# Forgetting attention's last output weights split ahead of its additions, norm factors spread by one operation and one float32 product, key rotation issued later

## The chip, the cores and the metric

One NeuronCore of a Trainium2 chip runs the whole network in one launch. The metric is the device time of the launch in microseconds; the median of several executions counts. TensorE (PE) multiplies, VectorE (DVE), ScalarE (ACT) and GpSimd (POOL) do the elementwise work, SyncE (SP) issues most transfers.

## The reference

Two layers over 512 tokens of width 1024, float32. Layer 0 is "Forgetting attention" (16 heads of 64, with a decay added to the scores), layer 1 latent attention (16 heads; queries from a latent of 768, keys and values from one of 256, and one rotated key of 64 shared by all heads). A feed-forward block with a convolution over time follows each. Every block begins with an RMS norm.

```python
def rmsnorm(x, g):
    xf = x.astype(jnp.float32)
    y = xf * lax.rsqrt(jnp.mean(xf * xf, axis=-1, keepdims=True) + EPS)
    return (y * g.astype(jnp.float32)).astype(x.dtype)
...
    for layer in range(DEPTH):
        if layer < N_A:
            x = x + fox_mixer(rmsnorm(x, fox_norm[layer]), ...)
        else:
            if layer == N_A:
                k_nope, k_rope, v = mla_shared_kv(x, kv_in_norm, w_dkv, kv_norm, w_uk, w_uv, cos, sin)
            x = x + mla_mixer(rmsnorm(x, mla_norm[j]), w_dq[j], q_norm[j], w_uq[j], ...)
        x = x + conv_ffn(rmsnorm(x, ffn_norm[layer]), ...)
    return rmsnorm(x, final_norm)
```

## The kernel before

Activations lie transposed, features on the 128 partitions and the 512 tokens along the free side, in 8 slabs of 128 features (`xT`). Every float32 operand of a large product is split into a high half (fp32r) and a low half, the rest; `mm3` (lines 83 to 85) makes one product of three: high by high, high by low, low by high. A tile of 128 output features over 1024 inputs is 8 steps of `mm3`, 24 products of 128x128 by 128x512.

Weights come through `load_w`: SP issues the transfer into `raw` (3 buffers), ACT casts the high half into `whi` (L104), DVE, or POOL with `eng=g`, subtracts for the low half `wlo` (L105). `whi` and `wlo` have 2 buffers each, so a tile's weights can be split only when the products of the tile two before are through. With a gain, POOL multiplies the raw weights first (L99).

A scheduler orders each engine's instructions from the program; every engine then runs its list strictly in order, and semaphores make it wait.

**Norms.** `Squares` adds up the squares of the slabs (L139 on ACT or L141 elsewhere, then L145). `rstd_of` sums over features with float32 products against two columns of ones (L153), scales (DVE, L156) and raises to -0.5 (POOL, L158). `bcast` spreads the 512 factors over all partitions: `bcast_ps` splits the factors in two halves (L165, L166), DVE multiplies the identity by each of the four columns of each half (L171, eight operations), and PE multiplies both by ones (L172). ACT copies the result (L179). The norm factor is applied to the result of a tile, not ahead of it (`Rstd.after`): the first tile's end issues the sum, the second's the spread, and tiles that wait for it stand in PSUM (`acc`, 3 buffers).

**Forgetting attention's output projection** is 8 tiles, `wo_tile(d)`. Seven steps of tiles 0 to 4 are done ahead, between the last heads, with weights in spare buffers. `out_proj` (L256) then ends each tile, adds it to `xT` (L264), splits the sum for the feed-forward block (`split_x`: ACT L188, DVE L189) and squares it on POOL, the last on ACT. Tiles 5, 6 and 7 load their weights there, through `whi` and `wlo`.

**Latent attention's entry** (from L633): six query-latent tiles with `down`, then the rotated key's (`wdkv_d[KL]`, called KL below), then two key-value latents. Between them stand the query norm's sum and spread, the latents' scaling and splitting (`latents`, L643, L188, L189), and the key's rotation: `swapped` (ACT, L650), three POOL operations (L751 to L753), a cast (ACT) and a subtraction (POOL). Then come the rotated query part of two heads (`mm_rope`, `turn`), the query tiles `proj_q`, the key tiles `proj_k`, and the first scores (L203).

## Time and profile before

| | us |
|---|---|
| median of 3 runs | 1399.91 (1399.19 to 1400.15) |
| profiled execution, its own time | 1404.06 |
| profiled execution, span of its instructions | 1401.7 |
| PE busy, products | 1371.8 |
| DVE busy | 879.4 |
| ACT busy | 646.4 |
| POOL busy | 281.4 |

The span runs from the first to the last instruction; the execution's own time has what lies around it too. Times of the trace are counted from the span's start. An engine is busy while an instruction of it runs; products are pipelined, so the starts of two products are closer together than one lasts. Line numbers are those of the printed kernel.

### The profile page before, as it was taken

How to read it: one execution, taken by the hardware profiler on the slowest of the kernel's cores; microseconds unless marked ns; L12 is line 12 of the kernel's file. 1: busy time of each engine (PE TensorE's matmuls, PEld its weight loads, DVE VectorE, ACT ScalarE, POOL GpSimd, SP SyncE). 2: the span in 40 equal slices, each digit the busy share in tenths (PEclk: the TensorE clock that was granted, in tenths of full speed). 3: DMA queues.
4: the chain of work that ended last, by engine and by line, in shares of the span. 5: the costliest groups of instructions: out<-in, count | busy, mean ns of one | idle time of the engine just before them, and what ended most of it. 6: DMA issues, size and time to landing. Idle time of an engine off the chain costs nothing.

```text
span 1401.7 us, 17314 instructions
## 1 busy us (share of the span) xinstructions
PE 1371.8 (98%) x6594; PEld 1150.3 (82%) x6594; DVE 879.4 (63%) x1466; ACT 646.4 (46%) x1115; POOL 281.4 (20%) x214
## 2 busy tenths in 40 slices
PE   8999999999999999999899999999999999999997
PEld 7988887788888888887688888888888888888886
DVE  6667786677777654534766565675467777774333
ACT  5588884344444432223456555653244444442111
POOL 4333323300000001244423222212210000000212
PEclk9999999999999999999899999999999999999998
DMA  5321121232232333332121111212322323232331
GB/s 181 104 77 63 57 68 48 90 103 92 96 100 92 104 93 86 100 115 80 42 68 50 62 56 49 76 56 90 105 90 92 104 90 105 91 101 85 98 102 68
DMA packets 41250, 120.21 MB, mean 86 GB/s; under 512 B 5552, under 2 KB 9952, under 8 KB 41168
## 3 DMA queue, kind: packets, MB, share of 16 engines
q1 hardware_dynamic: 39184, 117.00, 26.3%
q0 software_dynamic: 1840, 2.09, 0.6%
q8 instruction: 51, 0.84, 0.2%
q14 instruction: 31, 0.25, 0.1%
q10 hardware_dynamic: 144, 0.03, 0.0%
HBM read 116.74 MB, written 2.36 MB: 85 GB/s over the span
## 4 chain that ended last, share of the span: by engine, by line
PE 44%; DVE 3%; ACT 3%; issue 1%; POOL 0%; DVEq 0%; ACTq 0%
PE acc L84 13%; PE acc L83 13%; PE acc L85 13%; PE att L203 2%; PE acc L730 2%; ACT r L650 1%; ACT e L214 1%; PE att L237 1%; DVE Vp L712 1%; DVE ptl L241 0%; DVE tr L686 0%; DVE r L676 0%; ACT pth L240 0%; DVE r L672 0%; PE att L83 0%
## 5 line engine op out<-in xcount | busy, mean ns | idle before, releaser
L83 PE MATMUL acc<-big,whi 128*128 128x512 f32 (+1 forms) x1504 | 587.6, 391 | 2.7 <-ACT big L188 1.6
L85 PE MATMUL acc<-big,wlo 128*128 128x512 f32 (+1 forms) x1504 | 585.3, 389 | 3.5 <-DVE wlo L105 3.5
L84 PE MATMUL acc<-big,whi 128*128 128x512 f32 (+1 forms) x1504 | 585.5, 389 | 1.2 <-DVE big L189 1.2
L104 ACT CAST whi<-raw 128x1024 fp32r<-128x1024 f32 (+5 forms) x243 | 228.8, 945 | 413.8 <-PE acc L84 289.8
L85 PEld LDWEIGHTS acc<-big,wlo 128*128 128x128 f32 x1504 | 284.2, 189 | 63.0 <-DVE wlo L105 4.1
L83 PEld LDWEIGHTS acc<-big,whi 128*128 128x128 f32 x1504 | 284.0, 189 | 61.2 <-ACT big L188 3.0
L84 PEld LDWEIGHTS acc<-big,whi 128*128 128x128 f32 x1504 | 284.4, 189 | 59.7 <-DVE big L189 1.8
L105 DVE TENSOR_TENSOR wlo<-raw,whi 128x1024 fp32r<-128x1024 f32 (+3 forms) x179 | 232.6, 1299 | 138.6 <-ACT whi L104 136.0
L141 POOL TENSOR_TENSOR r<-xT 128x512 f32<-128x512 f32 x28 | 31.3, 1122 | 724.4 <-DVE xT L264 403.0
L105 POOL TENSOR_TENSOR wlo<-raw,whi 128x768 fp32r<-128x768 f32 (+3 forms) x64 | 107.1, 1677 | 248.3 <-ACT whi L104 135.8
L304 DVE SCALAR_TENSOR_TENSOR c<-u,conv,c 128x510 f32<-128x510 f32 (+1 forms) x176 | 131.1, 748 | 3.5 <-ACT c L302 0.6
L299 DVE TENSOR_TENSOR u<-acc,R 128x512 f32<-128x512 f32 x88 | 60.3, 687 | 76.3 <-PE acc L85 76.3
L214 ACT ACTIVATE e<-e,nm 128x128 f32<-128x128 f32 (+3 forms) x128 | 71.2, 557 | 42.8 <-DVE nm L208 42.8
L145 POOL TENSOR_TENSOR r<-r,r 128x512 f32<-128x512 f32 x38 | 72.5, 1908 | 28.9 <-ACT r L139 22.1
L302 ACT ACTIVATE c<-u,conv 128x512 f32<-128x512 f32 x88 | 71.4, 813 | 3.1 <-DVE u L299 2.7
L308 ACT ACTIVATE sg<-c 128x512 f32<-128x512 f32 x44 | 27.8, 632 | 78.8 <-DVE c L304 78.8
L185 ACT CAST big<-sg 128x512 fp32r<-128x512 f32 x32 | 19.9, 621 | 81.7 <-DVE sg L309 81.6
L217 DVE TENSOR_SCALAR e<-e,rl 128x128 f32<-128x128 f32 (+3 forms) x128 | 56.6, 506 | 1.1
L241 DVE TENSOR_TENSOR ptl<-att,pth 128x512 fp32r<-128x512 f32 (+3 forms) x128 | 53.7, 484 | 5.1 <-ACT pth L240 5.1
L240 ACT CAST pth<-att 128x512 fp32r<-128x512 f32 (+3 forms) x128 | 45.2, 441 | 6.6 <-PE att L237 5.7
L237 PE MATMUL att<-idf,e 128*128 128x128 f32 x320 | 43.4, 275 | 0.5
L237 PEld LDWEIGHTS att<-idf,e 128*128 128x128 f32 x320 | 36.8, 140 | 8.5 <-DVE nm L208 3.8
(183 smaller groups left out, 1460.2 us busy)
## 6 DMA issues: line engine op xcount, KB each, us to landing
raw<-in_wfi SPq DMA_DIRECT2D x88, 512.0 KB, 3.4
raw<-in_wfu SPq DMA_DIRECT2D x32, 512.0 KB, 3.5
raw<-in_wmo SPq DMA_DIRECT2D x16, 512.0 KB, 3.4
raw<-in_wfu SPq DMA_DIRECT2D x16, 384.0 KB, 3.1
raw<-in_wuqn SPq DMA_DIRECT2D x16, 384.0 KB, 3.0
raw<-in_wq SPq DMA_DIRECT2D x8, 512.0 KB, 3.4
raw<-in_wk SPq DMA_DIRECT2D x8, 512.0 KB, 3.4
raw<-in_wv SPq DMA_DIRECT2D x8, 384.0 KB, 3.1
```

Of the source, the lines that this page charges most:

```text
L83: pe.matmul(out, wh, xh, start=start, stop=False)
L84: pe.matmul(out, wh, xl, start=False, stop=False)
L85: pe.matmul(out, wl, xh, start=False, stop=stop)
L104: a.copy(hi[:, c], raw[:, c])
L105: (eng or v).tensor_tensor(out=lo[:, c], in0=raw[:, c], in1=f(hi[:, c]), op=ALU.subtract)
L145: (adder or g).tensor_tensor(out=self.sum, in0=self.sum, in1=sq, op=ALU.add)
L214: a.activation(es[i], es[i], AF.Exp, scale=-1.0, bias=nm[:, i:i + 1], accum_out=l[:, i:i + 1])
L217: v.tensor_scalar(out=es[i], in0=es[i], scalar1=rl[:, i:i + 1], scalar2=None, op0=ALU.mult)
L237: pe.transpose(out=pt[:, (i - j) * P:(i - j + 1) * P], in_=es[i][:, j * P:(j + 1) * P], identity=idf)
L299: v.tensor_tensor(out=u, in0=pt, in1=R, op=ALU.mult)
L302: a.activation(c, u, AF.Identity, scale=cw[:, 2:3], bias=cw[:, 3:4])
L304: v.scalar_tensor_tensor(out=c[:, s:], in0=u[:, :S - s], scalar=cw[:, 2 - s:3 - s], in1=c[:, s:], op0=ALU.mult, op1=ALU.add)
```

## The change

The output projection of the Forgetting attention ends tiles 0 and 1 first, then loads the weights of tiles 5 and 6 (`begun`; tile 5's low half on POOL), then goes on with tiles 2 to 4; its squares are all taken on ACT. A norm's factors are spread by one DVE operation, which multiplies the identity and the factors with broadcast views, and one float32 product against float32 ones. The sum and the spread of an entry norm are issued after 11 and 18 steps of `mm3`, in place of 8 and 16. In the latent attention the query norm's sum and spread are issued inside the key's tile and the first key-value tile, the latents come ahead of the key's rotation, the two key-value squares are summed by PE without an addition, and `turn` issues its DVE operation ahead of the ACT ones.

```diff
@@ -121,8 +121,8 @@
     v.memset(ones, 1.0)
-    ones_r = cp.tile([P, P], F32R, name="ones_r")
+    onesP = cp.tile([P, P], F32, name="onesP")
...
@@ -160,16 +160,10 @@
-        two = T(sp, [P, 2, NT], F32R, "two", 2)
-        rh, rl = two[:, 0, :m], f(two[:, 1, :m])
-        v.tensor_copy(rh, r)
-        v.tensor_tensor(out=rl, in0=r, in1=f(rh), op=ALU.subtract)
-        pt = att()[:, :m * P]
-        for j, part in enumerate((f(rh), rl)):
-            d = T(cp, [P, 512], F32R, "r2", R2)[:, :m * P]
-            for i in range(m):
-                v.tensor_scalar(out=d[:, i * P:(i + 1) * P], in0=idf, scalar1=part[:, i:i + 1], scalar2=None, op0=ALU.mult)
-            pe.matmul(pt, ones_r, d, start=(j == 0), stop=(j == 1))
+        d, pt = r2()[:, :m * P], att()[:, :m * P]
+        v.tensor_tensor(out=d.rearrange("p (i t) -> p i t", i=m), in0=idf.unsqueeze(1).to_broadcast([P, m, P]),
+                        in1=r.unsqueeze(2).to_broadcast([P, m, P]), op=ALU.mult)
+        pe.matmul(pt, onesP, d, start=True, stop=True)
         return pt
...
@@ -253,7 +247,7 @@
-    def out_proj(tile_of, gbase):
+    def out_proj(tile_of, gbase, eng=None):
...
@@ -263,25 +257,27 @@
             split_x(xs, d, xT[:, d, :], None if gbase is None else gain(gbase, d))
-            squares.add(xT[:, d, :], a if d == KD - 1 else g)
+            squares.add(xT[:, d, :], a if d == KD - 1 else (eng or g))
         return xs, squares
...
         def __init__(self, squares):
-            self.squares, self.step, self.R, self.todo = squares, 0, None, []
+            self.squares, self.steps, self.R, self.todo = squares, 0, None, []
+
+        def step(self):
+            self.steps += 1
+            if self.steps == KD + 3:
+                self.r = rstd_of([self.squares.sum], D)
+            if self.steps == 2 * KD + 2:
+                self.R = bcast(self.r)
+                for e in self.todo:
+                    e(self.R)
...
                 self.todo.append(evacuate)
-                if self.step == 0:
-                    self.r = rstd_of([self.squares.sum], D)
-                else:
-                    self.R = bcast(self.r)
-                    for e in self.todo:
-                        e(self.R)
-                self.step += 1
             else:
...
@@ -315,6 +311,7 @@
                         mm3(pt, (wh[:, k, :], wl[:, k, :]), parts(xs, k), k == 0, k == KD - 1)
+                        rstd.step()
                     rstd.after(lambda R, j=j, b=b, pt=pt: evacuate(j, b, pt, R))
...
@@ -576,7 +573,10 @@
-            loads = [(lambda c=c: load(c), KD // 2) for c in (0, 1)] if early else [(lambda: load_w(wfo_d[d], [P, KD, P]), KD)]
+            def whole():
+                return begun.pop(d) if d in begun else load_w(wfo_d[d], [P, KD, P])
+
+            loads = [(lambda c=c: load(c), KD // 2) for c in (0, 1)] if early else [(whole, KD)]
             return pt, out_tile(pt, loads, KD, lambda k: parts(oT, k))
...
@@ -588,7 +588,7 @@
         es = {0: scores(0)}
-        stream, ahead = fillers(), {}
+        stream, ahead, begun = fillers(), {}, {}
...
@@ -615,9 +615,12 @@
                 split_x(oT, h // 2, op_t, None)
-        fill((4,) * 7)
-
-        xs, squares = out_proj(lambda d: ahead[d] if d in ahead else wo_tile(d, acc(), False), G_FFN)
+        fill((4,) * 7 + (0, 1))
+        begun[5] = load_w(wfo_d[5], [P, KD, P], eng=g)
+        begun[6] = load_w(wfo_d[6], [P, KD, P])
+        fill((2, 3, 4))
+
+        xs, squares = out_proj(lambda d: ahead[d] if d in ahead else wo_tile(d, acc(), False), G_FFN, a)
...
@@ -630,11 +633,15 @@
-        def down(w_d, gbase, dst):
+        def down(w_d, gbase, dst, between=()):
             wh, wl = load_w(w_d, [P, KD, P], gain=(KD, gains[:, gbase:gbase + KD]))
             pt = acc()
+            between = dict(between)
             for k in range(KD):
                 mm3(pt, (wh[:, k, :], wl[:, k, :]), parts(xs, k), k == 0, k == KD - 1)
+                rstd.step()
+                if k in between:
+                    between[k]()
             rstd.after(lambda R: v.tensor_tensor(out=dst, in0=pt, in1=R, op=ALU.mult))
...
@@ -668,8 +675,8 @@
             c, t_ = r2(), r2()
+            v.scalar_tensor_tensor(out=c, in0=pt, scalar=MSCALE, in1=cosT, op0=ALU.mult, op1=ALU.mult)
             swapped(t_, pt, MSCALE)
-            v.scalar_tensor_tensor(out=c, in0=pt, scalar=MSCALE, in1=cosT, op0=ALU.mult, op1=ALU.mult)
...
@@ -736,33 +743,41 @@
             down(wdq_d[j], G_MLA, qc[:, j, :])
-            if j:
-                for i in ((0, 1) if j == 1 else (j,)):
+            if j > 1:
+                for i in ((0, 1, 2) if j == 2 else (j,)):
                     squares.add(qc[:, i, :], a, v if j == KQ - 1 else g)
...
         krt, krs = kr[:, 0, :], kr[:, 1, :]
-        down(wdkv_d[KL], G_KVIN, krt)
-        r = rstd_of([squares.sum], QL)
-        down(wdkv_d[0], G_KVIN, qc[:, KQ, :])
-        Rq = bcast(r, T(mp, [P, S], F32, "e3", 2))
+        norm = {}
+
+        def q_sums():
+            norm["q"] = rstd_of([squares.sum], QL)
+
+        def q_factors():
+            norm["R"] = bcast(norm["q"], T(mp, [P, S], F32, "e3", 2))
+
+        down(wdkv_d[KL], G_KVIN, krt, {2: q_sums})
+        down(wdkv_d[0], G_KVIN, qc[:, KQ, :], {0: q_factors})
+        Rq = norm["R"]
         latents(0, KQ - 2, Rq, G_Q)
+        down(wdkv_d[1], G_KVIN, qc[:, KQ + 1, :])
+        mask = T(cp, [P, S], F32, "R", 1)
+        nc.gpsimd.dma_start(mask, const_d[:, C_MM:C_MM + S])
+        kv_sq = []
+        for k in range(KL):
+            kv_sq.append(r2())
+            a.activation(kv_sq[k], qc[:, KQ + k, :], AF.Square)
+        latents(KQ - 2, 2, Rq, G_Q + KQ - 2)
+        end = turn(mm_rope(0))
+        r = rstd_of(kv_sq, KVL)
+        proj_q(0)
         swapped(krs, krt, 1.0)
...
         g.tensor_tensor(out=krt, in0=krt, in1=krs, op=ALU.add)
-        down(wdkv_d[1], G_KVIN, qc[:, KQ + 1, :])
-        mask = T(cp, [P, S], F32, "R", 1)
-        nc.gpsimd.dma_start(mask, const_d[:, C_MM:C_MM + S])
-        squares = Squares()
-        for k in range(KL):
-            squares.add(qc[:, KQ + k, :], a, v)
-        latents(KQ - 2, 2, Rq, G_Q + KQ - 2)
         a.copy(mr[:, 0, :], krt)
         g.tensor_tensor(out=mr[:, 1, :], in0=krt, in1=f(mr[:, 0, :]), op=ALU.subtract)
-        end = turn(mm_rope(0))
-        r = rstd_of([squares.sum], KVL)
-        proj_q(0)
         latents(KQ, KL, bcast(r, T(mp, [P, S], F32, "e3", 2)), G_KV)
```

DVE's list at the end of the Forgetting attention's output projection, before. `xT<-acc` and `xT<-att` are the additions of tiles 0, 1 (acc) and 2, 3, 4 (att), then 5; `wlo_2738` and `wlo_2775` are the low halves of tile 5's and tile 6's weights; `big_2689` are the splits of the sums.

```order
L264 TENSOR_TENSOR xT<-acc_2323,xT 128x512
L264 TENSOR_TENSOR xT<-acc_2393,xT 128x512
L105 TENSOR_TENSOR wlo_2738<-raw_2735,whi_2737 128x1024
L189 SCALAR_TENSOR_TENSOR big_2689<-xT,gains,big_2689 128x512 x2
L264 TENSOR_TENSOR xT<-att_2500,xT 128x512
L264 TENSOR_TENSOR xT<-att_2607,xT 128x512
L264 TENSOR_TENSOR xT<-att_2655,xT 128x512
L189 SCALAR_TENSOR_TENSOR big_2689<-xT,gains,big_2689 128x512 x3
L105 TENSOR_TENSOR wlo_2775<-raw_2772,whi_2774 128x1024
L264 TENSOR_TENSOR xT<-acc_2734,xT 128x512
```

The same list after, with the line numbers of the changed kernel; `wlo_2692` is tile 6's low half, `wlo_2800` tile 7's.

```order
L258 TENSOR_TENSOR xT<-acc_2311,xT 128x512
L258 TENSOR_TENSOR xT<-acc_2381,xT 128x512
L258 TENSOR_TENSOR xT<-att_2488,xT 128x512
L105 TENSOR_TENSOR wlo_2692<-raw_2689,whi_2691 128x1024
L183 SCALAR_TENSOR_TENSOR big_2704<-xT,gains,big_2704 128x512 x2
L258 TENSOR_TENSOR xT<-att_2595,xT 128x512
L183 SCALAR_TENSOR_TENSOR big_2704<-xT,gains,big_2704 128x512
L258 TENSOR_TENSOR xT<-att_2643,xT 128x512
L183 SCALAR_TENSOR_TENSOR big_2704<-xT,gains,big_2704 128x512 x2
L258 TENSOR_TENSOR xT<-acc_2734,xT 128x512
L105 TENSOR_TENSOR wlo_2800<-raw_2797,whi_2799 128x1024
```

Tile 5's low half is no longer on DVE (it is on POOL), and tile 6's stands after three additions, ahead of all splits, where it stood after five additions and five splits.

DVE's list around the latent attention's query norm, before. `kn_5599<-acc` takes the rotated key's tile out of PSUM, `wlo_5719` are low weights, `two`, `r_1114` and `r_1115` belong to the spread.

```order
L145 TENSOR_TENSOR r_1078_5449<-r_1078_5449,r_1099_5595 128x512
L638 TENSOR_TENSOR kn_5599<-acc_5607,R_5445 128x512
L156 TENSOR_SCALAR rstd_5638<-att_5633 128x4
L105 TENSOR_TENSOR wlo_5719<-raw_5715,whi_5718 128x1024
L165 CAST two_5675<-rstd_5638 128x4
L166 TENSOR_TENSOR two_5675<-rstd_5638,two_5675 128x4
L171 TENSOR_SCALAR r_1114_5679<-idf,two_5675 128x128 x4
L171 TENSOR_SCALAR r_1115_5685<-idf,two_5675 128x128 x4
L638 TENSOR_TENSOR big_5354<-acc_5648,R_5445 128x512
L643 TENSOR_TENSOR r_1116_5692<-big_5354,e_1111_5674 128x512
```

After, with `r_1106` the spread's operand:

```order
L145 TENSOR_TENSOR r_1076_5446<-r_1076_5446,r_1093_5559 128x512
L156 TENSOR_SCALAR rstd_5586<-att_5581 128x4
L164 TENSOR_TENSOR r_1106_5617<-idf,rstd_5586 128x512
L645 TENSOR_TENSOR kn_5563<-acc_5571,R_5423 128x512
L105 TENSOR_TENSOR wlo_5664<-raw_5660,whi_5663 128x1024
L650 TENSOR_TENSOR r_1108_5644<-big_5330,e_1105_5616 128x512
```

The sum's scaling and the spread's operand now stand ahead of the key's tile; on PE the sum (L153) stands behind 13 of the key tile's 24 products, where it stood behind all, and the spread's product 14 products after it, where it was 24.

POOL's list around the key-value norm, before: low weights of the first rotated query tile (`wlo_5768`), the mask's load, low weights of query tile 0 (`wlo_5808`) and 1 (`wlo_5869`), and the key-value norm's pow.

```order
L105 TENSOR_TENSOR wlo_5768<-raw_5765,whi_5767 128x768
L756 DMA R_5748<-in_const 128x512
L105 TENSOR_TENSOR wlo_5808<-raw_5805,whi_5807 128x768
L158 TENSOR_TENSOR rstd_5802<-rstd_5802,small 128x4
L105 TENSOR_TENSOR wlo_5869<-raw_5866,whi_5868 128x768
L105 TENSOR_TENSOR wlo_5897<-raw_5894,whi_5896 128x256
```

After, where `wlo_5812` is query tile 1:

```order
L105 TENSOR_TENSOR wlo_5710<-raw_5707,whi_5709 128x768
L105 TENSOR_TENSOR wlo_5754<-raw_5751,whi_5753 128x768
L766 DMA R_5693<-in_const 128x512
L105 TENSOR_TENSOR wlo_5812<-raw_5809,whi_5811 128x768
L158 TENSOR_TENSOR rstd_5748<-rstd_5748,small 128x4
L105 TENSOR_TENSOR wlo_5840<-raw_5837,whi_5839 128x256
```

The pow now stands behind the low weights of query tile 1.

## Rows read from the trace of the kernel before

**Rows 1.** The page, part 1: busy us, share of the span, instructions.
```profile
PE 1371.8 (98%) x6594; PEld 1150.3 (82%) x6594; DVE 879.4 (63%) x1466; ACT 646.4 (46%) x1115; POOL 281.4 (20%) x214
```
**Rows 2.** Waits of PE: engine, line, waited for: us in total, times, longest.
```profile
PE att L172 <- DVE r L171: 5.0, 5, 1.9
...
PE att L172 <- DVE zn L450: 0.4, 1, 0.4
PE att L153 <- POOL r L145: 0.4, 1, 0.4
```
**Rows 3.** Timeline of PE, latent attention: start, us, instruction [idle before <-releaser].
```profile
634.58 0.50 PE L172 MATMUL att<-r,ones_r 128*128 128x512 f32 x1 [1.39 <-DVE r L171]
...
657.24 0.39 PE L85 MATMUL acc<-big,wlo 128*128 128x512 f32 x1
...
662.90 0.83 PE L153 MATMUL att<-small,r 128*128 128x2 f32 x7
...
671.37 0.50 PE L172 MATMUL att<-r,ones_r 128*128 128x512 f32 x1 [1.24 <-DVE r L171]
...
704.32 2.08 PE L203 MATMUL att<-kn,tn 128*128 128x128 f32 x12
```
**Rows 4.** Timeline of PE, Forgetting attention's output projection and what follows.
```profile
235.87 0.39 PE L83 MATMUL acc<-big,whi 128*128 128x512 f32 x1
...
242.95 0.51 PE L83 MATMUL acc<-big,whi 128*128 128x512 f32 x1 [0.93 <-ACT whi L104]
247.00 0.80 PE L85 MATMUL acc<-big,wlo 128*128 128x512 f32 x1 [3.54 <-DVE wlo L105]
...
265.56 0.95 PE L153 MATMUL att<-small,r 128*128 128x2 f32 x8
```
**Rows 5.** One stretch: its us, busy us by engine, then PEclk, DMA share, GB/s.
```profile
248.00:252.00 4.00, 4.00 (x11) 3.11 (x10) 2.84 (x2) 0.30 (x1) 3.84 (x4) 0.50 0.67 248
```
**Rows 6.** Timeline of PE: four float32 products, and one spread's pair of products.
```profile
41.90 2.33 PE L463 MATMUL att<-e,z 128*16 128x512 f32 x8
44.16 0.44 PE L426 MATMUL acc<-whi,big 128*128 128x384 f32 x1
...
271.95 0.62 PE L172 MATMUL att<-r,ones_r 128*128 128x512 f32 x2
272.40 0.39 PE L83 MATMUL acc<-big,whi 128*128 128x512 f32 x1
```
**Rows 7.** Timeline of ACT and DVE in the same output projection.
```profile
233.12 1.05 ACT L104 CAST whi<-raw 128x1024 fp32r<-128x1024 f32 x1 [3.33 <-PE acc L84]
...
241.10 3.86 DVE L189 SCALAR_TENSOR_TENSOR big<-xT,gains,big 128x512 fp32r<-128x512 f32 x3
...
244.88 2.06 DVE L105 TENSOR_TENSOR wlo<-raw,whi 128x1024 fp32r<-128x1024 f32 x1
```
**Rows 8.** Groups by line, shapes apart: count, busy us, mean ns, idle before.
```profile
L105 POOL TENSOR_TENSOR wlo<-raw,whi 128x1024 fp32r<-128x1024 f32 x16 | 38.6, 2412 | 60.6 <-ACT whi L104 37.6 <-DVE ptl L241 23.1
...
L675 DVE TENSOR_TENSOR r<-r,sinT 128x512 f32<-128x512 f32 x8 | 5.5, 686 | 0.0
```
**Rows 9.** Instructions on the tile `two`: ns at least, median, at most.
```profile
L171 DVE TENSOR_SCALAR r<-idf,two x56: 273/280/1923, 29.8 to 1393.8; 128x128 fp32r<-128x128 f32 x56
```
**Rows 10.** Timeline of POOL and DVE at the latent attention's entry and its query norm.
```profile
630.66 1.03 POOL L158 TENSOR_TENSOR rstd<-rstd,small 128x4 f32<-128x4 f32 x1
...
632.54 1.90 POOL L99 TENSOR_TENSOR raw<-raw,gains 128x1024 f32<-128x1024 f32 x1 [0.84 <-DMA raw<-in_wdq]
...
659.79 0.69 DVE L145 TENSOR_TENSOR r<-r,r 128x512 f32<-128x512 f32 x1
...
664.13 2.06 POOL L158 TENSOR_TENSOR rstd<-rstd,small 128x4 f32<-128x4 f32 x1 [6.69 <-DVE rstd L156]
```
**Rows 11.** The chain that ended last, at the end: start, us, what.
```profile
1392.89 0.18 DVE two L165
...
1393.79 0.90 PE att L172 x2
```

More of the change, by code (lines that the diff above doesn't have):

```diff
@@ L123, in tile_kernel @@
     v.memset(ones, 1.0)
-    ones_r = cp.tile([P, P], F32R, name="ones_r")
-    v.memset(f(ones_r), 1.0)
+    onesP = cp.tile([P, P], F32, name="onesP")
+    v.memset(onesP, 1.0)
     v.memset(mhalf, -0.5)
```

## The prediction

> **What bounds the kernel now.** The page first: TensorE (PE) is busy 98% of the span [rows 1], so the time is PE's work plus the places where PE stands still. Then PE's waits: two products of the helper that spreads norm factors (L172) wait five times for the DVE lines that fill their operand, 5.0 us in all, once 0.4 us for another DVE operation, and one norm sum waits 0.4 us for POOL [rows 2]. Then PE's timeline, for what a stretch costs beyond its work. A 128x512 product is issued every 0.226 us: from 657.24 to 662.90 there are 25 of them [rows 3]. The Forgetting attention's output tiles 5, 6, 7 and the first tile behind them are 4x24 = 96 products, 21.7 us; they run from 235.87 to 265.56, 29.69 us [rows 4]. So **7.95 us** are lost there. About 4.5 us is idle time: 0.93 before the product at 242.95 and 3.54 before the one at 247.00, which wants the low half of tile 6's weights [rows 4]. The rest, 3.5 us, is refill and the clock: right behind that standstill the granted clock is 0.50, the lower of its two levels, 1.2 of 2.4 GHz [rows 5]. In the latent attention, the stretch from the key-rotation tile (657.47) to the first scores (704.32) takes 46.85 us [rows 3]. Its work is 138 products (72 for three down tiles, 18 for rope 0, 36 for two query tiles, 12 for two key tiles), 31.25 us, two norm sums of 0.83 [rows 3] and two spreads of 0.45 [rows 6]: 33.8 us. There PE waits for a spread operand, then for latents, and loses about 13 us.
>
> **The change part by part.** *Out-projection.* Before, DVE takes tile 6's low half after five additions and five splits: it starts at 244.88 and takes 2.06, behind three splits of 3.86 us [rows 7]. After, DVE's list puts it behind the third addition. Tile 5's low half goes to POOL, all squares to ACT. Worked forward: ACT casts tile 5's high half at 233.12 for 1.05 [rows 7], POOL needs 2.41 for this shape [rows 8], so the low half is there at 234.2+2.4 = 236.6. PE wants it with the third product, at 235.87+2x0.226 = 236.3: 0.3 us of waiting. Tile 6's low half starts on DVE when tile 2's addition is through (about 235.5) and is there by 238, even if it first stands behind POOL until 236.6. PE wants it near 242: 4 us of room. Tile 7's is next late: ACT's cast now stands behind five pairs of split and square, which wait for DVE's additions. I place the cast at 244 to 246 and the low half at 246 to 248; PE wants it at 236.2+48x0.226+0.45 = 247.5. Hence 0.3 more. Gain 7.95-0.6 = **7.35** (bounds: 5.2, with 0.8 and 2 us of waiting, to 7.95).
>
> *The spread.* Removed per spread: a cast, a subtraction, eight 128x128 multiplies; added: one 128x512 product of two SBUF operands on DVE, of which another such line takes 0.69 [rows 8]; from above it is that behind a POOL instruction, 1.92 [rows 9] and 0.69. I take 0.7, since POOL mostly has nothing to do just then. On PE two products become one in full float32. The trace has no 128-row one of 512 columns. The nearest: four float32 products of 512, 384, 256 and 128 columns, from 41.90 to 44.16 [rows 6], 1.77 ns a column, so 0.90 us for 512. From below it is one ordinary product, 0.23, from above the same price at the lower clock level, 1.8. I take 0.90, since PE is busy around five of the six. The pair it replaces took 271.95 to 272.40, 0.45 [rows 6]. So each of six full spreads costs PE **0.45 more** wherever PE did not wait. That is paid in both feed-forward entries: -0.9. What hides DVE's op there is two tiles of PE's products. In the value projection the 0.4 us wait [rows 2] pays for it: 0.
>
> Costed at nothing: the first three query latents' squares are taken one tile later, on ACT and POOL that wait there, and the mask's load goes behind one more weight split on POOL; should either be late, the query sum waits for it, and the 0.6 of room below is gone first.
>
> *Rstd by steps.* The sum moves from 8 steps behind the entry to 11, the spread from 16 to 18. At the latent attention's entry, waits of 1.39 [rows 3] and 0.4 [rows 2] go, less 0.45: **1.35**. Check: the sum is at 627.9+0.8; POOL's pow follows its weight multiply, which before ended at 630.66, and takes 1.03 [rows 10]; the spread is on DVE at 631.6 to 632.3; PE comes at about 633.5. Room 1.2 us.
>
> *Latent norms and key rotation.* The query sum is ready at 659.79+0.69 = 660.5 [rows 10]; PE's list has it behind 13 products of the rotation tile, at 660.4. Pow is then alone (1.03), the spread op done at about 663.9, and PE reaches its product 14 products after the sum, at 664.5. Before it came at 671.37 [rows 3]. The latents start some 5 us earlier, and DVE no longer spends 5 us on multiplies. Rope 0 begins at about 675.6. Its low weights are on POOL behind the rotated key, whose sub waits for ACT's cast, which waits for POOL's three ops: done at 676.2 to 676.6 against a need of 676.1, so 0.4. The key-value sum lies inside rope 0; but POOL now holds the low half of query tile 1 ahead of the pow (its list above), and that cast waits for rope 0's end to free its buffer: pow ends at about 685.4, the spread at 686.2, PE comes at 685.8: 0.5 with the hop. Behind it the two key-value latents are split on ACT and DVE just as PE wants them: 0.8. The key-value squares are no longer added by DVE; PE sums both, which doubles that sum. Floor 31.25+3x0.83+2x0.90 = 35.55, gain at best 46.85-35.55 = 11.3, less 1.7: **9.6** (bounds: 6.3, with 5 us of waits, to 11.3). With the waits short, the lower clock does not come back.
>
> *Tail.* Between DVE's 1392.89 and the last pair lies 0.90 [rows 11]; the new op of half width needs about 0.4 and a hop: +0.36. The float32 product costs 0.2 to 0.45 more than the pair of 0.90 [rows 11], and the half before it 0.2 more: -0.15 (bounds -0.4 to +0.2).
>
> Sum: 7.35+1.35+9.6+0-0.9-0.15 = 17.25 us. The profiled execution took 1404.06, 0.3% over the median of 1399.91; the terms are microseconds of either. **1399.9-17.25 = 1382.6.** The bounds give 5.2+0.1+6.3-0.9-0.4 = 10.3 and 7.95+1.35+11.3-0.9+0.2 = 19.9 (0.1 at the latent entry: a spread that stands 1.2 behind POOL), so 1380 to 1389.6.
>
> **The rivals.**
> *A, the forecast* (1380 to 1386): 0.66.
> *B, the spread op stands behind POOL* (0.08). One of the 56 multiplies took 1.92 us where the median is 0.28 [rows 9], as long as POOL's weight multiply of 1.90 then running, and a pow that takes 1.03 alone took 2.06 behind a DVE op [rows 10]. If the spread op starts just after POOL's next instruction, it loses 1.9: at the latent entry 1.9-1.2 = 0.7, at the key-value spread 0.8, for tile 7's low half 1: a sum of 14.75 in place of 17.25, 1385.1. Against it: POOL's next multiply there waited for its data until 632.54 [rows 10]. By the Trainium skill (SBUF — State Buffer, "Who interferes with whom") a VectorE instruction with two SBUF inputs and a GpSimd one that reads SBUF lock each other out for a whole instruction, whoever issued first. The trace agrees with it in those two rows; by the rule alone, with all three meeting POOL, the sum is B's 14.75.
> *C, the wait comes back at tile 7* (0.08): ACT's squares hold its cast. It decides when the low half comes after about 250.5: then the wait is as long as before's 3.5, the clock falls again, and the whole 7.35 goes: 1390.
> *D, the latent chain* (0.10): ACT stands at the cast of the rotated key until POOL is through, with rope 0's weights and the latents behind it. Some 5 us more of waits, and the lower clock behind them: 1387.6.
> *E, nothing* (0.04): the waits move to equally late neighbours; 1398 to 1402. Against it: the waits end with the very lines that move.
> *F, slower* (0.04): the one wide op reads both operands with broadcast strides, which no DVE row shows. With rooms of about 2, 1.2, 0.6, 0, 2 and 2.7 us at the six full spreads, it must take over 5.2 us to lose 17.25+2.8; at 5.5 it loses 6.5x(5.5-0.7)-8.5 = 22.7 (the tail's two count as half a full one, on the path once): 1405. From below it is 0.69; nothing of this size is above 2 us in the rows.
>
> **How the numbers follow.** Time 1382.6 for A, the likeliest. A, B, D and part of C lie in 1379 to 1389: 0.84 and more. From no change this kernel's measurement tells about 0.2% (2.8 us). Faster: A to D, 0.92. Same 0.04 and slower 0.04 from E and F.
>
> **What would show it.** Right: no wait of PE over 1 us near 242 to 247 and granted clock 1.00 there; tile 6's low half on DVE before 239; one float32 record group at each spread taking 0.9; scores starting about 18 us earlier than 704.3. Wrong: a wait near 247 for the last low half, a spread waiting over 1 us behind POOL, a wide op over 2 us, or a clock near 0.5 around the key-value spread.

## The result, and the profile after

The changed kernel takes **1386.45 us** (median of 4 runs, 1384.77 to 1387.18) against 1399.76 for the kernel before (4 runs): ratio 0.9904, 95% interval 0.9886 to 0.9921, a gain of 13.3 us (11.1 to 16.0). The forecast was 1382.6 in a range of 1379 to 1389, with a chance of 0.92 for faster. The sign and the range held; the time lies just outside the 1380 to 1386 given to its likeliest case, A, and the sum was 3.9 us too large.

The page of the changed kernel, part 1, answers to [rows 1]:

```profile
PE 1362.4 (98%) x6602; PEld 1145.5 (83%) x6602; DVE 867.8 (63%) x1400; ACT 650.6 (47%) x1122; POOL 272.7 (20%) x208
```

Its waits of PE (engine, line, waited for: us in total, times, longest) answer to [rows 2]:

```profile
PE acc L85 <- POOL wlo L105: 2.0, 2, 1.7
PE att L166 <- DVE r L164: 1.6, 1, 1.6
...
PE acc L84 <- DVE big L183: 0.6, 2, 0.4
PE att L166 <- DVE z L444: 0.4, 1, 0.4
```

Of the spread's five waits for its operand, one of 1.6 us is left, in the tail. The 3.5 us for tile 6's low half are gone, and 1.7 us for a low half on POOL are new. The wait of 0.4 in the first norm is still there: it is for a DVE line that writes `z`, not for the operand.

PE's timeline in the output projection and at the feed-forward entry's spread (start, us, instruction [idle before <-releaser]) answers to [rows 4] and [rows 6]:

```profile
237.59 0.39 PE L83 MATMUL acc<-big,whi 128*128 128x512 f32 x1
...
238.49 0.50 PE L85 MATMUL acc<-big,wlo 128*128 128x512 f32 x1 [0.29 <-POOL wlo L105]
...
254.56 0.39 PE L83 MATMUL acc<-big,whi 128*128 128x512 f32 x1
...
267.76 1.02 PE L166 MATMUL att<-r,onesP 128*128 128x512 f32 x2
268.21 0.80 PE L83 MATMUL acc<-big,whi 128*128 128x512 f32 x1
268.85 0.40 PE L84 MATMUL acc<-big,whi 128*128 128x512 f32 x1
```

Three tiles of 24 products now take 254.56-237.59 = 16.97 us, 0.7 over their work of 16.3. DVE takes tile 6's low half ahead of all splits, 0.56 us before tile 5's first product, where in [rows 7] it took it 9.0 us behind that product of [rows 4]:

```profile
237.03 2.48 DVE L105 TENSOR_TENSOR wlo<-raw,whi 128x1024 fp32r<-128x1024 f32 x1
```

The granted clock stays at the upper level where [rows 5] show 0.50 (the stretch, then PE, PEld, DVE, ACT and POOL busy, clock, DMA share, GB/s):

```profile
246.00:250.00 4.00, 4.00 (x19) 3.17 (x18) 4.00 (x4) 3.23 (x5) 3.05 (x3) 1.00 0.00 0
250.00:254.00 4.00, 4.00 (x19) 3.30 (x18) 3.48 (x4) 1.32 (x3) 1.43 (x2) 1.00 0.49 142
```

The table cuts the span of each profiled execution at the same places of PE's timeline: the first norm (its sum to the value projection's first L83), the output projection (tile 5's first product to the feed-forward block's first), that block (to the latent attention's first product), the latent entry (to the rotated key's tile), the latent norms (to the first scores), the head loop with its output projection (to the second block's first product), that block (to the final norm's sum) and the tail (to the end). Each number is a difference of two starts; the rest of a span is the first loads, 27.2 to 29.8 us in a way that goes with no edit, and the first attention's products, 174.9 to 175.0 in all.

| kernel | span | first norm | out-proj. | block 0 | latent entry | latent norms | head loop | block 1 | tail |
|---|---|---|---|---|---|---|---|---|---|
| before, profiled first | 1401.7 | 33.67 | 24.25 | 360.44 | 36.90 | 46.86 | 322.69 | 357.72 | 16.97 |
| before again | 1398.9 | 33.65 | 23.62 | 360.44 | 34.88 | 44.12 | 323.06 | 357.72 | 16.99 |
| output projection alone | 1390.5 | 33.68 | 16.96 | 360.44 | 34.91 | 42.77 | 323.10 | 357.72 | 17.05 |
| spread alone | 1399.0 | 34.31 | 23.06 | 360.90 | 35.10 | 44.12 | 323.18 | 358.17 | 16.25 |
| `turn` alone | 1391.9 | 33.65 | 23.07 | 360.45 | 34.82 | 42.65 | 319.94 | 357.71 | 16.99 |
| output projection and `turn` | 1385.1 | 33.66 | 16.99 | 360.45 | 35.05 | 40.55 | 320.41 | 357.72 | 16.95 |
| changed | 1384.1 | 34.28 | 16.97 | 360.91 | 34.49 | 39.65 | 319.94 | 358.17 | 16.38 |
| changed, again | 1386.0 | 34.28 | 17.00 | 360.90 | 34.50 | 39.65 | 319.90 | 358.18 | 16.81 |
| changed, `turn` undone | 1385.8 | 34.27 | 16.97 | 360.90 | 34.50 | 38.61 | 323.26 | 358.17 | 16.89 |
| changed, query norm late | 1385.0 | 34.29 | 16.98 | 360.90 | 34.50 | 40.37 | 320.08 | 358.17 | 16.75 |
| changed, rope 0's low half on DVE | 1385.7 | 34.29 | 16.97 | 360.90 | 34.50 | 41.58 | 320.09 | 358.17 | 16.83 |
| changed, old spread | 1383.6 | 33.68 | 16.99 | 360.45 | 35.03 | 38.62 | 320.12 | 357.72 | 17.38 |
| changed, old spread in first norm and blocks | 1383.5 | 33.68 | 16.97 | 360.45 | 34.50 | 39.63 | 319.99 | 357.72 | 16.47 |
| changed, old spread there and in the latent norms | 1383.6 | 33.67 | 16.99 | 360.45 | 34.50 | 39.24 | 320.14 | 357.72 | 16.21 |

### The profile page after: what moved, and what is told of

The parts are those of the page before. It is cut to its first block, busy times and chain, and to the rows that moved or that the text cites. A ratio compares the mean times of both kernels' runs of the same rounds, so it can differ in the third digit from the quotient of the medians.

```text
span 1384.1 us, 17267 instructions
## 1 busy us (share of the span) xinstructions
PE 1362.4 (98%) x6602; PEld 1145.5 (83%) x6602; DVE 867.8 (63%) x1400; ACT 650.6 (47%) x1122; POOL 272.7 (20%) x208
## 4 chain that ended last, share of the span: by engine, by line
PE 90%; DVE 4%; ACT 3%; issue 1%; POOL 1%; DMA 0%; SPq 0%; DVEq 0%; POOLq 0%; ACTq 0%
PE acc L83 26%; PE acc L85 26%; PE acc L84 26%; PE att L197 4%; PE att L231 2%; PE acc L737 2%; PE acc L565 1%; ACT r L657 1%; ACT e L208 1%; DVE Vp L719 1%; PE att L83 1%; PE att L85 1%; PE att L84 1%; DMA xT<-in_xT 0%; PE att L153 0%
## 5 line engine op out<-in xcount | busy, mean ns | idle before, releaser
L83 PE MATMUL acc<-big,whi 128*128 128x512 f32 (+1 forms) x1504 | 586.9, 390 | 0.0
L83 PEld LDWEIGHTS acc<-big,whi 128*128 128x128 f32 x1504 | 282.5, 188 | 57.7 <-issue 1.2
L105 POOL TENSOR_TENSOR wlo<-raw,whi 128x256 fp32r<-128x256 f32 (+3 forms) x65 | 109.3, 1686 | 260.4 <-ACT whi L104 152.9
L141 POOL TENSOR_TENSOR r<-xT 128x512 f32<-128x512 f32 x21 | 21.9, 1041 | 700.2 <-DVE xT L258 380.4
L208 ACT ACTIVATE e<-e,nm 128x128 f32<-128x128 f32 (+3 forms) x128 | 71.2, 557 | 36.5 <-DVE nm L202 36.3
L231 PE MATMUL att<-idf,e 128*128 128x128 f32 x320 | 40.3, 272 | 0.0
```

Source lines behind the costliest of these rows:

```text
L83: pe.matmul(out, wh, xh, start=start, stop=False)
L105: (eng or v).tensor_tensor(out=lo[:, c], in0=raw[:, c], in1=f(hi[:, c]), op=ALU.subtract)
L208: a.activation(es[i], es[i], AF.Exp, scale=-1.0, bias=nm[:, i:i + 1], accum_out=l[:, i:i + 1])
L231: pe.transpose(out=pt[:, (i - j) * P:(i - j + 1) * P], in_=es[i][:, j * P:(j + 1) * P], identity=idf)
```

## The experiments

### The kernel before once more

No edit. 

> The kernel before, once more, unchanged. Two theories on the 2.75 us that the head loop of the latent attention gave and that the forecast had at 0. Turn: the changed order in `turn` gives them, so this run shows 31.4 us for a pair of heads as the first profile did. Oddity: the profiled execution of before was slow by itself (its own time is 4.3 us over the median), so this run shows 31.0 for a pair and a time of 1399 to 1400.

Measured: 1401.31 us, where 15 runs of this kernel beside it have a median of 1400.97. Two starts of scores, one pair of heads apart (PE's timeline; in the first row the window's edge cuts the count, not the start), are 31.42 us apart, as in the first profile:

```profile
777.03 0.44 PE L203 MATMUL att<-kn,tn 128*128 128x128 f32 x3
...
808.45 2.07 PE L203 MATMUL att<-kn,tn 128*128 128x128 f32 x12
...
811.64 1.78 PE L237 MATMUL att<-idf,e 128*128 128x128 f32 x10
813.18 0.36 PE L707 MATMUL acc<-whi,big 128*128 128x256 f32 x1
```

So the oddity theory falls for the head loop. It holds elsewhere: the latent entry takes 34.88 in place of 36.90, the latent norms 44.12 in place of 46.86. At the latent entry the spread's eight multiplies take 1.65 us, and PE's pair comes without a wait. In the first profile (second fence) they took 3.29, since one of them stood behind the weight multiply of [rows 10] and took 1.92 [rows 9]; here POOL's next one starts only at 635.47, when its data has landed.

```profile
633.18 1.65 DVE L171 TENSOR_SCALAR r<-idf,two 128x128 fp32r<-128x128 f32 x8
635.47 1.90 POOL L99 TENSOR_TENSOR raw<-raw,gains 128x1024 f32<-128x1024 f32 x1 [2.61 <-DMA raw<-in_wdq]
634.57 0.82 PE L172 MATMUL att<-r,ones_r 128*128 128x512 f32 x2
```

```profile
632.01 3.29 DVE L171 TENSOR_SCALAR r<-idf,two 128x128 fp32r<-128x128 f32 x8
```

In the latent norms the granted clock tells the two executions apart. Two stretches of the first profile, then one of this one, then the same place in the run with the output projection's part alone, whose instructions there are the same:

```profile
684.00:688.00 4.00, 4.00 (x13) 3.32 (x14) 1.47 (x5) 0.41 (x1) 1.48 (x1) 0.50 0.06 18
688.00:692.00 4.00, 4.00 (x15) 3.22 (x14) 0.05 (x1) 3.19 (x5) 1.84 (x1) 0.76 0.00 0
```

```profile
684.00:688.00 4.00, 4.00 (x12) 3.13 (x11) 1.09 (x3) 0.83 (x1) 1.03 (x1) 0.59 0.00 0
```

```profile
677.00:681.00 4.00, 4.00 (x19) 3.31 (x18) 0.94 (x3) 2.34 (x4) 2.39 (x2) 1.00 0.00 0
```

With the clock never down in it, the stretch from the rotated key's tile to the first scores takes 42.77 in that run.

### The output projection's part alone

```diff
...
-            squares.add(xT[:, d, :], a if d == KD - 1 else g)
+            squares.add(xT[:, d, :], a if d == KD - 1 else (eng or g))
...
+        fill((4,) * 7 + (0, 1))
+        begun[5] = load_w(wfo_d[5], [P, KD, P], eng=g)
+        begun[6] = load_w(wfo_d[6], [P, KD, P])
+        fill((2, 3, 4))
...
```

> The kernel before with the output projection's part alone (tiles 0 and 1 ended first, weights of tiles 5 and 6 begun, tile 5's low half on POOL, squares on ACT). Forecast's term: 7.35 us faster, 1392.4; from tile 5's first product to the feed-forward block's first 22.4 us in place of 29.7. Rival: without the other parts the wait comes back at tile 7 and the gain is under 4 us.

Measured: 1392.52 us, ratio 0.9951 (0.9938 to 0.9965). From tile 5's first product (237.55) to the block's norm sum (259.95), the 96 products that the expectation means, it takes 22.40; the three tiles alone take 16.96. Executions of the old output projection need 23.06 to 24.25 for these (two of them have 6.8 us at the lower clock there, the other two 3.4), so the part is worth 6.1 to 7.3, by itself and within the whole change alike. The rival falls. Which of the part's four edits (order of the tiles, weights begun early, tile 5's low half on POOL, squares on ACT) gives how much, no run tells.

### The spread alone

```diff
...
-        for j, part in enumerate((f(rh), rl)):
...
-            pe.matmul(pt, ones_r, d, start=(j == 0), stop=(j == 1))
...
+        v.tensor_tensor(out=d.rearrange("p (i t) -> p i t", i=m), in0=idf.unsqueeze(1).to_broadcast([P, m, P]),
+                        in1=r.unsqueeze(2).to_broadcast([P, m, P]), op=ALU.mult)
+        pe.matmul(pt, onesP, d, start=True, stop=True)
```

> The kernel before with the new spread alone (one DVE operation, one float32 product). By the forecast's terms: at the two feed-forward entries 0.45 lost each, at the latent entry and the value projection the waits of 1.39 and 0.4 shrink by about 1.3 (a 0.7 operation in place of eight multiplies) and pay 0.45; in the latent norms up to 3 us gained, since two waits for the operand shorten by about 1.5 each: 1396 to 1399. Rival: the spread alone costs, since every product is 0.45 dearer and what DVE gives back was not waited for: 1401 to 1402.

Measured: 1400.11 us, ratio 0.9997 (0.9988 to 1.0006): nothing. The blocks lose 0.46 and 0.45, as expected, and the first norm 0.66; the tail gains 0.74. The expected gain in the latent norms isn't there (44.12 both times): PE's waits of 0.21 and 1.24 for the query spread's operand go, but it then waits 0.80, 0.57, 0.28 and 0.40 for latents; and the key-value spread's operand stands on DVE behind `turn`'s product, which idles 6.12 us for ACT's swaps, at a granted clock down to 0.50. My expectation is wrong in that, and the rival's slower time too.

### One line of `turn`

```diff
+            v.scalar_tensor_tensor(out=c, in0=pt, scalar=MSCALE, in1=cosT, op0=ALU.mult, op1=ALU.mult)
             swapped(t_, pt, MSCALE)
-            v.scalar_tensor_tensor(out=c, in0=pt, scalar=MSCALE, in1=cosT, op0=ALU.mult, op1=ALU.mult)
```

> The kernel before with one line moved: in `turn` the DVE product with the cosines is issued ahead of ACT's four swaps. Turn theory: a pair of heads takes 31.0 in place of 31.4 us, the kernel is 2.5 to 3 us faster, 1397. Rival: no change within 0.5 us, 1399.5, and a pair takes what it takes in the kernel before.

Measured: 1394.61 us, ratio 0.9960 (0.9948 to 0.9973), a gain of 5.6 (3.8 to 7.3), more than the theory's 2.5 to 3. The head loop takes 319.94 in place of 323.06, as the theory has it; the latent norms, which it left out, take 42.65 in place of 44.12, both with 3.4 us at the lower clock. PE in one pair of heads, to be read against the fence of the kernel before above:

```profile
772.21 0.61 PE L203 MATMUL att<-kn,tn 128*128 128x128 f32 x4
...
803.18 2.07 PE L203 MATMUL att<-kn,tn 128*128 128x128 f32 x12
...
806.38 1.25 PE L237 MATMUL att<-idf,e 128*128 128x128 f32 x10
807.38 0.36 PE L707 MATMUL acc<-whi,big 128*128 128x256 f32 x1
```

A pair takes 30.97, and from the transposes (L237) to the next products it is 1.00 in place of 1.54. The chain of work that ended last says why. In the kernel before (first profile) it runs from ACT's last swap over the product with the cosines and the scores' maximum (L208, both on DVE) to the exponentials on ACT; in the changed kernel it goes from the last swap straight to the exponentials (L208 there):

```profile
813.54 0.60 ACT r L650
814.16 0.56 DVE r L672
814.72 0.05 issue
814.77 0.28 DVE e L208
815.09 1.58 ACT e L214 x6
```

```profile
795.77 0.70 DVE r L678
796.47 0.02 issue
796.50 0.59 ACT r L657
...
798.30 0.59 ACT r L657
798.89 0.03 issue
798.91 1.50 ACT e L208 x5
```

Both DVE's product and ACT's swaps read the same rotated query tile in PSUM, and whichever is issued second waits for the other. Last, the product held the maximum behind it; first, it costs the swaps 0.50 us (ACT's row at 804.11 in this run). From the first swap to the exponentials it is 798.91-796.50 = 2.41 in place of 815.09-811.74 = 3.35 (before, the first swap of that pair starts at 811.74, ahead of the first fence): 0.94-0.50 = 0.44 for each of the loop's seven rotated pairs, 3.1 in all, where 3.12 are found. Rotated pair 0 stands ahead of the key-value spread's operand in the same way; with the clock at the upper level throughout, `turn` is worth 2.2 there in the old order (42.77 with the output projection's part alone, 40.55 in the next run).

### These two together

```diff
+        begun[5] = load_w(wfo_d[5], [P, KD, P], eng=g)
+        begun[6] = load_w(wfo_d[6], [P, KD, P])
...
+            v.scalar_tensor_tensor(out=c, in0=pt, scalar=MSCALE, in1=cosT, op0=ALU.mult, op1=ALU.mult)
             swapped(t_, pt, MSCALE)
```

> The kernel before with the output projection's part and the one line of `turn`, nothing else. Theory: the two add up, 6.7 for the one and 4.6 for the other (3.1 in the head loop, 1.5 ahead of the first scores): 1389.5, so that the steps of the entry norms, the new spread and the new order in the latent norms together are worth 3 us. Rival: with the clock undisturbed in the latent norms the two alone give 1387 and the rest nothing.

Measured: 1388.13 us, ratio 0.9910 (0.9897 to 0.9924), beside 0.9895 (0.9881 to 0.9910) for the changed kernel run again in the same comparison (1386.60). Between theory and rival: the spread, the steps and the whole new order of the latent attention add some 1.5 us, which the two intervals hardly tell from nothing. By the table they give 0.9 in the latent norms, 0.55 at the latent entry, 0.5 in the loop and 0.1 to 0.6 in the tail, and take 0.6, 0.45 and 0.45 in the first norm and the blocks: 0.5 to 1 in all.

> The changed kernel once more, unchanged, beside the next three: 1385 to 1387.

Measured: 1386.60 us, as expected, and the latent norms take 39.65 once more.

### The changed kernel with one part taken back

`turn` back in its old order:

```diff
-            v.scalar_tensor_tensor(out=c, in0=pt, scalar=MSCALE, in1=cosT, op0=ALU.mult, op1=ALU.mult)
             swapped(t_, pt, MSCALE)
+            v.scalar_tensor_tensor(out=c, in0=pt, scalar=MSCALE, in1=cosT, op0=ALU.mult, op1=ALU.mult)
```

> The changed kernel with the two lines of `turn` back in their old order (ACT's four swaps ahead of DVE's product). Turn theory, after the run with that line alone: a pair of heads takes 31.41 again in place of 30.96, some 3.1 us over the loop, and DVE's product waits for the swaps ahead of the key-value spread's operand, 1.5 to 2.4 us more: 1391 to 1392. Rival: in the changed kernel the spread's operand no longer stands behind that product, so only the loop's 3.1 come back: 1389.5.

Measured: 1388.00 us, ratio 0.9910 (0.9895 to 0.9924). The loop loses 3.3, but the latent norms take 38.61, 1.04 less than with the new order, which neither theory had. DVE's timeline shows the place: here the key-value latents are scaled at 681.81, ahead of the first split of the rotated query (L693, 683.12), and their splits end at 685.25, 36.38 behind the start of the rotated key's tile; in the changed kernel they come behind that split and end at 687.61, 37.65 behind that start, and PE waits twice for them (0.42 and 0.18).

The query norm's sum and spread behind whole tiles, as before:

```diff
-        down(wdkv_d[KL], G_KVIN, krt, {2: q_sums})
-        down(wdkv_d[0], G_KVIN, qc[:, KQ, :], {0: q_factors})
+        down(wdkv_d[KL], G_KVIN, krt, {KD - 1: q_sums})
+        down(wdkv_d[0], G_KVIN, qc[:, KQ, :], {KD - 1: q_factors})
```

> The changed kernel with the query norm's sum behind the whole rotated-key tile and its spread behind the whole first key-value tile, as before the change; everything else as changed. Theory: the latents start 3 to 4 us later and PE waits 3 us more ahead of or inside rope 0: 1389 to 1390, first scores some 3 us later after the key's tile. Rival: the lists had that room, and only `turn` matters: 1386.5.

Measured: 1387.54 us, ratio 0.9904 (0.9889 to 0.9919), and from the rotated key's tile to the first scores 40.37: 0.7 us in place of 3. The wait moved, and the two intervals do not tell the times apart. In the changed kernel the latents are early enough to meet the key's rotation; POOL, DVE and PE there:

```profile
661.01 1.70 POOL L776 TENSOR_TENSOR kn<-kn,cosT 128x512 f32<-128x512 f32 x1 [5.63 <-ACT kn L657]
662.68 1.73 POOL L777 TENSOR_TENSOR kn<-kn,sinT 128x512 f32<-128x512 f32 x1
664.50 1.62 POOL L778 TENSOR_TENSOR kn<-kn 128x512 f32<-128x512 f32 x1
...
668.38 4.51 POOL L105 TENSOR_TENSOR wlo<-raw,whi 128x768 fp32r<-128x768 f32 x2
661.72 4.94 DVE L183 SCALAR_TENSOR_TENSOR big<-r,gains,big 128x512 fp32r<-128x512 f32 x3 [0.15 <-ACT big L182]
670.69 0.50 PE L85 MATMUL acc<-big,wlo 128*128 128x512 f32 x1 [1.71 <-POOL wlo L105]
```

With the late spread POOL is alone, and rope 0's low weights are in time, but the latents are not:

```profile
660.19 1.29 POOL L777 TENSOR_TENSOR kn<-kn,sinT 128x512 f32<-128x512 f32 x1
661.56 1.27 POOL L778 TENSOR_TENSOR kn<-kn 128x512 f32<-128x512 f32 x1
...
664.81 2.32 POOL L105 TENSOR_TENSOR wlo<-raw,whi 128x768 fp32r<-128x768 f32 x1
669.00 0.50 PE L84 MATMUL acc<-big,whi 128*128 128x512 f32 x1 [0.80 <-DVE big L183]
```

Three splits take 4.94 us beside three POOL operations of 1.6 to 1.7, where one alone takes 0.74 and a rotation operation alone 1.29. The Trainium skill (SBUF — State Buffer, "Who interferes with whom") says that the two engines share a pair of ports under an exclusive lock; the trace agrees, with the two lists going forward in turns: POOL's three start at 661.02, 662.68 and 664.50, DVE's at 661.72, 663.19 and 664.89. Both read two tiles in SBUF here, the case that the prediction quoted; of the two rows that it set beside the rule, the pow's is of that kind, and the other is a multiply by a scalar column.

Rope 0's low weights on DVE:

```diff
-            return mm_lat(load_w(wuqr_d[j], [P, KQ, P], eng=g), 0, KQ)
+            return mm_lat(load_w(wuqr_d[j], [P, KQ, P], eng=g if j else None), 0, KQ)
```

> The changed kernel with the low half of rope 0's weights on DVE in place of POOL. Theory: PE's wait of 1.71 us for it goes, since DVE takes it at about 667.6, ahead of the need at 668.8; 1.5 us faster than the changed kernel, 1384.9. Rival: DVE's latents behind it come later by one operation of 0.9 us and PE waits for them instead: no change within 0.5 us.

Measured: 1386.59 us, ratio 0.9896 (0.9881 to 0.9910): the rival, by its time. By its cause only in part: PE's 1.71 shrinks to 0.31, a latent's split is late by 1.11, and the waits of 0.42 and 0.18 behind the key-value spread are gone, so there is less waiting in all (1.42 in place of 2.31). But in the profiled execution the clock then falls for 6.8 us, and the stretch takes 41.58; what the edit is worth with the clock up isn't shown:

```profile
668.33 0.50 PE L85 MATMUL acc<-big,wlo 128*128 128x512 f32 x1 [0.31 <-DVE wlo L105]
672.01 0.50 PE L83 MATMUL acc<-big,whi 128*128 128x512 f32 x1 [1.11 <-ACT big L182]
```

```profile
673.00:677.00 4.00, 4.00 (x17) 3.52 (x17) 0.77 (x2) 0.75 (x1) 0.00 (x0) 0.57 0.03 10
677.00:681.00 4.00, 4.00 (x12) 3.10 (x12) 1.37 (x4) 2.43 (x5) 2.82 (x2) 0.58 0.12 33
```

### The old spread, where and where not

Everywhere:

```diff
...
-        pe.matmul(pt, onesP, d, start=True, stop=True)
...
+        for j, part in enumerate((f(rh), rl)):
...
+            pe.matmul(pt, ones_r, d, start=(j == 0), stop=(j == 1))
```

> The changed kernel with the old spread everywhere (two fp32r products, ten DVE operations). Theory: the new spread costs 0.45 at each feed-forward entry and 0.65 in the first norm, gains 0.6 to 0.7 in the tail, and about as much as it costs in the latent norms, where the issue order has given it room: 1385 to 1387 for the changed kernel's 1386.45. Rival: without the one operation the eight multiplies meet POOL and the latent norms wait 3 us more: 1389 to 1390.

Measured: 1384.30 us, ratio 0.9878 (0.9861 to 0.9894): faster than the changed kernel by its median, with intervals that overlap. First norm, blocks and tail are as expected; the latent norms take 38.62, 1.0 less, and PE's wait for rope 0's low weights is 1.08 there. They do so although the granted clock falls in them (first row), which it does neither in the changed kernel nor in the last run of this section (second row; columns as above):

```profile
675.00:679.00 4.00, 4.00 (x13) 3.21 (x12) 0.80 (x3) 3.18 (x5) 2.81 (x2) 0.57 0.15 50
```

```profile
675.00:679.00 4.00, 4.00 (x20) 3.25 (x20) 1.08 (x3) 2.82 (x5) 2.07 (x2) 1.00 0.31 98
```

In the first norm and the two blocks alone (`old=True` takes the old lines; one tile of ones serves both products):

```diff
-                R = bcast(rs)
+                R = bcast(rs, old=True)
...
-            rstd = Rstd(squares)
+            rstd = Rstd(squares, True)
```

> The changed kernel, with the old spread (two fp32r products) in the first norm and in both feed-forward entries, where PE does not wait for its operand, and the new one at the latent entry, in the latent norms and in the tail. Theory: 0.6 in the first norm and 0.45 at each feed-forward entry come back, the rest stays: 1.5 us faster than the changed kernel, 1384.9. Rival: the first norm waits for the eight multiplies instead and only 0.9 come back.

Measured: 1385.31 us, ratio 0.9887 (0.9871 to 0.9902). The places give back 0.60, 0.46 and 0.45, the expected 1.5; the latent norms stay at 39.63.

In the two latent norms as well:

```diff
-            norm["R"] = bcast(norm["q"], T(mp, [P, S], F32, "e3", 2))
+            norm["R"] = bcast(norm["q"], T(mp, [P, S], F32, "e3", 2), old=True)
```

> The same with the old spread in the two latent norms as well, so that only the latent entry and the tail have the new one. Theory, from the run with the old spread everywhere, whose stretch from the rotated key's tile to the first scores took 38.4 us in place of 39.4: 1 us faster again, 1384. Rival: that 1 us was chance of where POOL and DVE met, or the lower clock comes back there: the same as the kernel before it in this list, or 1 us slower.

Measured: 1385.00 us, ratio 0.9882 (0.9868 to 0.9897), latent norms 39.24: 0.4 of the 1 us. With the clock up, PE reaches the key-value spread earlier and waits 0.63 and 0.69 for its multiplies, which it did not with the clock down. The three versions with old spreads lie 1.1 to 2.3 us under the changed kernel's two medians; their stretches say that they beat it, and the timing alone doesn't settle it. So the new spread gives nothing or takes, but for the tail and, together with the new steps, the latent entry.

## Why the prediction was right, and where its sum was not

Its terms, in us gained, against the table:

| term | forecast | from the first profile | from before again |
|---|---|---|---|
| output projection | 7.35 | 7.28 | 6.65 |
| spread in the first norm | 0 | -0.61 | -0.63 |
| spread in the two blocks | -0.9 | -0.92 | -0.92 |
| latent entry | 1.35 | 2.41 | 0.39 |
| latent norms | 9.6 | 7.21 | 4.47 |
| head loop | none | 2.75 | 3.12 |
| tail | -0.15 | 0.59 | 0.61 |
| first loads and first attention | none | -1.11 | 1.11 |
| sum | 17.25 | 17.6 | 14.8 |

Without the line on the first loads, which goes with no edit, the last column is 13.7, beside 13.3 by the medians.

*Output projection:* right in mechanism and size: no wait over 0.3 us, the granted clock at 1.00, tile 6's low half begun at 237.03; tile 7's low half, rival C's, caused no wait. The wide operation takes 0.69 and the float32 product costs 268.85-267.76-0.226 = 0.86 in all, forecast 0.7 and 0.90; so the blocks' -0.9 is right too, and rival F falls.

*"The terms are microseconds of either"* is the step that failed. The profiled execution was 4.2 us over the median, and the stretches that the terms were taken from were longer in it than in the second one (1401.31, itself 1.4 over): by 2.0 at the latent entry, 2.7 in the latent norms, 0.6 in the output projection. The first loads were 2.2 shorter. The text itself read [rows 9] and [rows 10] as a meeting of DVE and POOL, made it a rival with 0.08, and still booked the wait of 1.39 that it caused as a steady gain.

*Latent norms:* mis-sized beyond that. The sum and the spread did come early, as forecast; the scores start at 689.61, 14.7 us earlier than in the first profile, where 18 were forecast. But the loss of 1.7 above the floor of 35.55 became 4.1: rope 0's low weights wait 1.71 in place of 0.4. (Recorded waits make 2.3 of the 4.1; the rest lies in products that start more than 0.226 behind one another with no wait recorded.) That is rival D's place, the rotated key on POOL ahead of those weights, and B's cause, at about half of D's price; its clock did not fall. Taking the early query norm back costs only 0.7, since another wait takes over. The 9.6 was booked for the new order and the new spread, and the runs give these little: of the 7.21 by the first profile, 2.7 are that execution's own, 1.35 went with the lower clock that the second one still had (44.12 to 42.77), 2.2 come from `turn`'s line (42.77 to 40.55), and 0.9 is left (40.55 to 39.65), by one or two executions each.

*Latent entry:* in the second execution of the kernel before, PE waits 0.39 there, for the norm's sum, and no longer for the spread. With the new steps and the old spread the entry takes 35.03, with the new spread alone 35.10, with both 34.50.

*Head loop:* `turn`'s line had no term at all, and of the parts that were tried alone it is the second largest gain. The chain of work that ended last in the first profile passes through L650 and L672 in each of the seven rotated pairs, and on through L208 in six of them; a line that the diff touches stood in it, and I read the chain only at the tail.

*First norm:* the wait there was said to pay for the dearer product; it is for `z`, and stays. *Tail:* the sign was wrong; the half spread gives 0.1 to 0.8 by the runs of the table, and its operand's wait fell from 1.9 to 1.6. Rival F's "over 5.2 us" is 5.1 by its own sum.

So the range held by luck in part, through two errors of opposite sign: by the last column, some 6 us too much in the latent attention's entry and norms and 3 too little in its loop. Two things stay open: why the clock fell behind waits of 0.31 and 1.11 with DVE's weights and of 1.08 and 0.20 with the old spread, and not behind one of 1.71 in the changed kernel; and how much of the 1.0 us that the old spread gives in the latent norms is chance. The key's rotation, "issued later", moves nothing: with these lines ahead of the second key-value tile, as before, every engine has the same list.

## What to carry to other kernels

Before a wait is booked as a gain, see whether a second execution of the same kernel has it; here the profiled run was some us over the median, and its excess lay in two stretches with odd waits, which were the ones that the forecast was made from. Hold every line of a diff against the chain of work that ended last: a line that two engines share and that stands there in each turn of a loop is worth its step times the turns, however small it looks. In the first norm and the two blocks an operation that was cheaper on an engine nobody waited for bought nothing, and the dearer product on the bound engine was paid in full. And look at the granted clock of a stretch before its length is compared: in six of these fourteen profiles 3.4 to 10.2 us at the lower level lie in the latent norms.

## What was not expected of the hardware

The same instructions, in the same order, took 42.8 to 46.9 us in one stretch of three executions, by where POOL and DVE met and whether the granted clock fell (1.00, 0.59 or 0.50 at the same place). A float32 product of 512 columns delays the product behind it as well: it is issued 0.45 after it, and the next 0.64 later, where 0.226 is usual.
